# Four convolution taps per channel from TensorE to VectorE, and five weight splits from VectorE to ScalarE and accumulating DMAs

## The chip, the core and the metric

The kernel runs on one core of a Trainium2 chip. The core has a matrix engine (TensorE, "PE" in the profile, with its weight loads as "PEld"), a vector engine (VectorE, "DVE"), an engine for activation functions (ScalarE, "ACT"), a general engine (GpSimd, "POOL") and a synchronisation engine (SyncE, "SP"). SP, ACT and POOL issue DMA transfers, which 16 DMA engines carry out between the chip's main memory (DRAM) and the on-chip memory (SBUF). TensorE's results go into accumulator memory (PSUM), which the kernel uses as eight banks of 128 partitions by 512 numbers of f32. Each engine runs its own list of instructions in order and waits on semaphores for the others.

The metric is the device time of one execution in microseconds, as a median over runs.

## The reference

One transformer block over 256 tokens with 1024 features, all in f32. Attention and a depthwise convolution run side by side on the normalised input, their outputs are joined and projected, and a gated feed-forward layer follows.

```
u = rms_norm(x, mix_norm_g)
q, k, v, glu_a, glu_g = split(u @ w_in)                # 5 x 512 columns
attn_out = causal attention, 8 heads of 64, relative position bias
y = glu_a * sigmoid(glu_g)
y = depthwise causal convolution(y, 31 taps per channel) + b_dw    # 512 channels
conv_out = silu(layer_norm(y))
h = x + concat(attn_out, conv_out) @ w_out
u = rms_norm(h, ffn_norm_g)
h = h + (silu(u @ w_gate) * (u @ w_up)) @ w_down       # 1024 -> 2816 -> 1024
out = rms_norm(h, final_norm_g)
```

With 256 tokens and blocks of 256, each query only sees its own block, so the selection of blocks in the reference has no effect.

## The kernel before

**Split products.** Every large product is made of three TensorE passes in the type f32r. An f32 operand is split into an upper part, which is the operand rounded to f32r, and a lower part, which is what the rounding left. For weights the upper part is `wh`, made from the loaded tile `raw` on ScalarE (the step `h`, function `high`), and the lower part is `wl = raw - wh`, made by a subtraction on VectorE (the step `w`, function `split`, which makes the upper part too where no `h` came before). The input has the parts `uh` and `ul`. The passes are `wh*uh`, `wh*ul` and `wl*uh`. A weight load is a pair of tiles of 128 partitions by 1024 columns, numbered 0 and 1, so that the step `w.v1.0` splits the first tile of the second load of value weights. The names of loads are `a0`, `a1` (the convolution's inputs), `qk0` to `qk3`, `v0`, `v1`, `o0` to `o3` (the output projection), and then `g`, `u`, `d` for the feed-forward layer.

**Memory for weights.** There are six `raw` tiles, so that a load waits until the tiles of three loads earlier are read for the last time. `wl` is one region with nine slots that are used in turn, and there are nine `wh` tiles.

**The convolution.** It has two halves of 256 channels, and each half has two chunks of 128 channels, called j = 0 and 1. The first 20 taps (4*Q with Q = 5) run on TensorE. For that the gated input is stored to DRAM and read back four times with shifts of one token, so that 32 channels times four taps fill the 128 partitions (`ustk`). A stationary operand `wstk` of 128 rows by 32 columns holds the four taps of 32 channels, and one matmul with 256 moving columns adds four taps for 32 channels. `wstk` is built by VectorE in the step `cw`. One chunk takes Q passes times four groups of 32 channels, which is 20 matmuls, into the bank `pc` (the steps `c.half.j`). The other 11 taps (`ONV`) run as single instructions of 128 by 256: tap 0 on ScalarE (step `ca`), taps 1 to 10 as a fused multiply-add on VectorE into `cacc` (steps `ct.half.from.to`). The step `co` adds `pc` to `cacc` and sums the two chunks into `s4` ("s" in the profile) for the layer norm. `l.1` and `l.2` finish the sum, take the mean over channels with a matmul (`pm`) and subtract it from `cacc`.

**Attention.** `qk.hp.j` multiplies for a pair of heads, `qo` scales the result out of PSUM on VectorE, `sc` makes the scores (`ps`), `t` adds the bias and takes the row minimum on VectorE (`lg`, `mn`) and the exponential on ScalarE (`p`), `n` normalises, `fl` transposes on TensorE (`pt`), `fo` copies the transposes (`pts`). The value product is `v.0` to `v.3` (`pv`): `v.2` reads the tile `v1.0`, and `v.3` the tile `v1.1`. `pv.hp` multiplies with the values (`po`), and `mo.hp` splits the result into `mh` on ScalarE and `ml` on VectorE. The output projection `o.k` (`py`) takes 24 matmuls for each k. `o.0` and `o.1` read `o0.0` and `o0.1`, and `o.2` reads `o1.0`.

**What sets the order.** The string `PROGRAM` lists the steps of this part by hand, and each step appends its instructions to the lists of the engines that it uses. All engines keep this order. After it comes the feed-forward loop (`pf`, `pd`), which makes up the rest of the time. There the transfers of POOL move the activations through DRAM (`fd`, `fb`, `hd`, `ht`). In the stage that the change touches, POOL issues no transfer after the two stores of the gated input (`ud`) until the feed-forward layer, and SP issues all weight loads.

## Time and profile before

| | |
|---|---|
| time, median of 3 runs | 283.68 us (283.18 to 284.09) |
| the profiled execution: its time | 283.44 us |
| the profiled execution: its span from first to last instruction | 281.7 us |
| busy: TensorE, VectorE, ScalarE, GpSimd | 273.3, 203.0, 156.4, 43.6 us |
| granted TensorE clock, mean | 0.996 |
| DMA | 63.73 MB, mean 226 GB/s |

All places in time are microseconds from the start of the span of the profiled execution. In a row of the timeline the columns are start, duration, engine, line, operation, output and inputs, shapes, and the number of instructions merged into the row. In square brackets stands the idle time of the engine ahead of the row and what ended it. The start of a row reaches a little into the row before, since instructions overlap, so the pace of an engine is read from the starts. A matmul with f32 operands that aren't f32r, as in the convolution, shows as two records. The windows view gives the busy time of each engine in a stretch of time with the number of instructions, the granted clock, the mean busy share of the DMA engines and their rate.

The steps that the change touches lie between 44 and 86 us.

### The profile page before, as it was taken

The page shows a single profiled execution, that of the slowest core. Times are in us where ns is not written, and L with a number is a line of the kernel's source. Part 1 is how long each engine was busy: PE and PEld are TensorE (multiplying, and loading weights), DVE is VectorE, ACT ScalarE, POOL GpSimd, SP SyncE. Part 2 cuts the span into 40 slices and gives each one's busy share as a digit, 9 for nine tenths or more (in the row PEclk, how much of TensorE's full clock was granted, in tenths as well). Part 3 has the DMA queues.
Part 4 walks back from the last instruction along what each step waited for, and adds up shares of the span by engine and source line. Part 5 has one row for each costly group of instructions (what it writes and reads, how often), then busy time and mean ns, then how long its engine had stood idle before and what let it go on. Part 6 is the DMA issues. An engine that isn't in the chain of part 4 may idle for free.

```text
span 281.7 us, 4726 instructions
## 1 busy us (share of the span) xinstructions
PE 273.3 (97%) x1717; PEld 243.1 (86%) x1717; DVE 203.0 (72%) x375; ACT 156.4 (56%) x272; POOL 43.6 (15%) x80
## 2 busy tenths in 40 slices
...
GB/s 204 364 406 321 278 252 244 357 264 78 0 152 284 110 202 155 303 354 245 340 314 205 323 153 323 285 255 399 245 226 245 308 143 329 158 77 0 0 67 82
DMA packets 22089, 63.73 MB, mean 226 GB/s; under 512 B 3178, under 2 KB 5938, under 8 KB 22066
## 3 DMA queue, kind: packets, MB, share of 16 engines
q1 hardware_dynamic: 18754, 54.94, 59.2%
...
q8 instruction: 13, 0.21, 0.3%
...
## 4 chain that ended last, share of the span: by engine, by line
PE 82%; DVE 9%; issue 3%; DMA 1%; ACT 1%; SPq 1%; POOLq 0%; POOL 0%; DVEq 0%; ACTq 0%
PE pf L74 38%; PE pd L74 18%; PE pqk L74 8%; PE py L74 8%; PE pa L74 3%; PE pg L74 3%; DVE cacc L85 3%; DVE wl L85 2%; PE pc L74 2%; DMA raw_a<-in_w_in 1%; DVE acch L85 1%; PE pv L74 1%; DVE ht L85 1%; PE pt L77 1%; DVE lg L85 1%
## 5 line engine op out<-in xcount | busy, mean ns | idle before, releaser
L74 PE MATMUL pf<-wl,us 128*128 128x512 f32 x176 | 66.7, 379 | 0.0
L74 PE MATMUL pf<-wh_u,us 128*128 128x512 f32 x176 | 54.4, 379 | 0.0
L74 PE MATMUL pf<-wh_g,us 128*128 128x512 f32 x176 | 54.2, 379 | 0.0
L85 DVE TENSOR_TENSOR ff<-fs,pf 128x256 f32<-128x256 f32 x22 | 9.1, 420 | 49.4 <-ACT fs L85 49.4
L85 ACT ACTIVATE fs<-pf,rc_h 128x256 f32<-128x256 f32 x22 | 10.3, 473 | 60.8 <-PE pf L74 59.4
L74 PEld LDWEIGHTS pf<-wl,us 128*128 128x128 f32 x176 | 33.3, 189 | 4.7
L74 PEld LDWEIGHTS pf<-wh_g,us 128*128 128x128 f32 x176 | 33.3, 189 | 4.7
L74 PEld LDWEIGHTS pf<-wh_u,us 128*128 128x128 f32 x176 | 33.3, 189 | 4.7
L74 PE MATMUL pd<-wh_d,fh 128*128 128x512 f32 x84 | 32.0, 381 | 0.0
L74 PE MATMUL pd<-wh_d,fl 128*128 128x512 f32 x84 | 31.9, 380 | 0.0
L74 PE MATMUL pd<-wl,fh 128*128 128x512 f32 x84 | 31.8, 379 | 0.0
...
L85 DVE TENSOR_TENSOR wl<-raw_u,wh_u 128x1024 fp32r<-128x1024 f32 x22 | 26.3, 1219 | 4.9 <-ACT wh_u L85 4.9
L85 ACT CAST wh_u<-raw_u 128x1024 fp32r<-128x1024 f32 x22 | 22.6, 1045 | 11.1 <-PE pf L74 9.0
L85 DVE TENSOR_TENSOR wl<-raw_g,wh_g 128x1024 fp32r<-128x1024 f32 x22 | 25.9, 1217 | 1.1 <-ACT wh_g L85 1.0
L85 DVE TENSOR_TENSOR wl<-raw_d,wh_d 128x1024 fp32r<-128x1024 f32 x22 | 25.6, 1203 | 0.5 <-ACT wh_d L85 0.5
L85 ACT CAST wh_g<-raw_g 128x1024 fp32r<-128x1024 f32 x22 | 21.9, 1044 | 0.0
L85 ACT CAST wh_d<-raw_d 128x1024 fp32r<-128x1024 f32 x22 | 21.8, 1041 | 0.0
L74 PE MATMUL pqk<-us,wh_qk 128*128 128x256 f32 x128 | 21.7, 276 | 0.0
L74 PEld LDWEIGHTS pqk<-us,wh_qk 128*128 128x128 f32 x128 | 19.5, 192 | 0.5 <-issue 0.4
L74 PEld LDWEIGHTS pd<-wh_d,fl 128*128 128x128 f32 x84 | 15.9, 189 | 2.4 <-DVE fl L85 0.2
L74 PE MATMUL py<-mh,wh_o 128*128 128x256 f32 x64 | 18.0, 281 | 0.0
...
## 6 DMA issues: line engine op xcount, KB each, us to landing
...
```

Of the source, the lines that this page charges most:

```text
L74: return tc.keep_in_program_order(nc.tensor.matmul(*args, **kw))
L77: return tc.keep_in_program_order(nc.tensor.transpose(o, i, ident))
L85: return lambda *a, **k: tc.keep_in_program_order(f(*a, **k))
```

## The change

The first half of the convolution runs four passes of four taps on TensorE (16 taps) in place of five (20 taps). The four taps per channel that are left over run on VectorE, as eight more multiply-adds of 128 by 256 (four taps for two chunks). The second half stays as it was. The table of tap columns grows by four taps, so that its load has 172 columns in place of 156, and `wstk` of the first half is built with 512 columns per chunk in place of 640.

Five weight tiles (`v1.0`, `v1.1`, `o0.0`, `o0.1`, `o1.0`) get their lower parts by a new step `x` (`split_by_dma`). ScalarE makes the upper part as before. Then it writes the negated raw tile into the tile's slot of `wl`. The slot has the type f32r, so that what stands there is the negated upper part. Then a DMA that POOL issues adds the raw tile to it, which gives `raw - wh`. The five subtractions on VectorE are gone. The steps stand in the program one after the other behind `w.qk3.1`, where before only `h.v1.0` stood; the others were spread up to `w.o1.0`.

The place in the program where VectorE finishes the first half of the convolution, begins the second, and goes on to the logits of the third pair of heads (`lg`). `upad_81` and `upad_82` are the gated inputs of the two halves. Before:

```order
L85 SCALAR_TENSOR_TENSOR cacc<-upad_81,pv,cacc 128x256 x2
L85 TENSOR_TENSOR cacc<-pc_712,cacc 128x256 x2
L85 TENSOR_TENSOR s_149<-cacc 128x256
L85 TENSOR_TENSOR wl<-raw_v_0_609,wh_v_0_833 128x1024
L85 TENSOR_TENSOR wl<-raw_v_1_610,wh_v_1_834 128x1024
L85 SCALAR_TENSOR_TENSOR cacc<-upad_82,pv,cacc 128x256 x4
L85 TENSOR_TENSOR qk_918<-pqk_860,rb 128x512
L85 TENSOR_TENSOR wl<-raw_o_0_806,wh_o_0_887 128x1024
L85 TENSOR_TENSOR wstk_84<-pv 128x640 x2
L85 SCALAR_TENSOR_TENSOR cacc<-upad_82,pv,cacc 128x256 x4
L85 ISA lg_952,mn_953<-ps_940,bias 128x128
```

And in the changed kernel:

```order
L86 SCALAR_TENSOR_TENSOR cacc<-upad_81,pv,cacc 128x256 x10
L86 TENSOR_TENSOR cacc<-pc_712,cacc 128x256 x2
L86 TENSOR_TENSOR s_149<-cacc 128x256
L86 SCALAR_TENSOR_TENSOR cacc<-upad_82,pv,cacc 128x256 x4
L86 TENSOR_TENSOR qk_925<-pqk_864,rb 128x512
L86 TENSOR_TENSOR wstk_84<-pv 128x640 x2
L86 SCALAR_TENSOR_TENSOR cacc<-upad_82,pv,cacc 128x256 x4
L86 ISA lg_962,mn_963<-ps_950,bias 128x128
```

Eight more taps stand ahead of the sum with `pc`, and three subtractions are gone, two of them ahead of the scaling of `qk` and one behind it.

The place where VectorE goes from the layer norm's sum to the lower parts of the attention output (`ml`), which the output projection waits for. Before:

```order
L85 TENSOR_TENSOR s_149<-cacc 128x256
L85 TENSOR_TENSOR s_149<-s_149 128x256
L85 TENSOR_SCALAR vt<-pv_843,rc_x 128x512
L85 TENSOR_TENSOR wl<-raw_o_1_807,wh_o_1_888 128x1024
L85 TENSOR_TENSOR cacc<-cacc,pm 128x256 x4
L85 TENSOR_TENSOR wl<-raw_o_0_856,wh_o_0_1049 128x1024
L85 TENSOR_TENSOR ml<-po_1116,mh 128x256
```

And in the changed kernel:

```order
L86 TENSOR_TENSOR s_149<-cacc 128x256
L86 TENSOR_TENSOR s_149<-s_149 128x256
L86 TENSOR_SCALAR vt<-pv_847,rc_x 128x512
L86 TENSOR_TENSOR cacc<-cacc,pm 128x256 x4
L86 TENSOR_TENSOR ml<-po_1121,mh 128x256
```

The other two subtractions stood between the sum and `ml`, and are gone.

The place on ScalarE between the transposes of the first two pairs of heads and the exponentials of the third (`p`). Before:

```order
L85 CAST wh_v_0_833<-raw_v_0_609 128x1024
L85 CAST wh_v_1_834<-raw_v_1_610 128x1024
L85 CAST wh_o_0_887<-raw_o_0_806 128x1024
L85 CAST wh_o_1_888<-raw_o_1_807 128x1024
L85 ACTIVATE p_956,sm<-lg_952,mn_953 128x128
```

And in the changed kernel:

```order
L86 CAST wh_v_0_825<-raw_v_0_609 128x1024
L86 ACTIVATE wl<-raw_v_0_609 128x1024
L86 CAST wh_v_1_826<-raw_v_1_610 128x1024
L86 ACTIVATE wl<-raw_v_1_610 128x1024
L86 CAST wh_o_0_889<-raw_o_0_798 128x1024
L86 ACTIVATE wl<-raw_o_0_798 128x1024
L86 CAST wh_o_1_890<-raw_o_1_799 128x1024
L86 ACTIVATE wl<-raw_o_1_799 128x1024
L86 CAST wh_o_0_927<-raw_o_0_860 128x1024
L86 ACTIVATE wl<-raw_o_0_860 128x1024
L86 ACTIVATE p_966,sm<-lg_962,mn_963 128x128
```

Five negations are new, one behind each cast, and the cast of `o1.0` has moved up here from behind the third pair's normalisation. On POOL the five accumulating DMAs stand behind the two stores of the gated input, and ahead of the power function of the convolution's layer norm (`rc_ln`).

The diff; the host code changes only in the number of tap columns that it lays out:

```diff
-ONV = TAPS - 4 * Q
+QH = (4, 5)
+ONV = TAPS - 4 * min(QH)
...
-c.0.0 ct.0.6.7 h.qk3.0 w.v0.0 n.0 n.1 c.0.1 w.v0.1 h.qk3.1 w.qk3.0 ct.0.7.8 ct.0.8.10 qk.2.1 qo.2 ld.o0 fl.0 fo.0 fl.1 fo.1 w.qk3.1 h.v1.0 ct.0.10.11 co.0 w.v1.0
-v.0 ld.o1 qk.3.0 h.v1.1 w.v1.1 h.o0.0 ct.1.1.3 qk.3.1 qo.3 h.o0.1 w.o0.0 cw.1.0 cw.1.1 ct.1.3.5 v.1 sc.2 sc.3 t.2 t.3 ld.o2
-c.1.0 ct.1.5.7 n.2 n.3 c.1.1 ct.1.7.9 ct.1.9.11 h.o1.0 co.1 l.1 v.2 v.3 fl.2 fl.3 vt w.o0.1 fo.2 fo.3 l.2 ld.o3 w.o1.0
+c.0.0 ct.0.6.7 h.qk3.0 w.v0.0 n.0 n.1 c.0.1 w.v0.1 h.qk3.1 w.qk3.0 ct.0.7.8 ct.0.8.10 qk.2.1 qo.2 ld.o0 fl.0 fo.0 fl.1 fo.1 w.qk3.1 x.v1.0 x.v1.1 ct.0.10.15 co.0
+v.0 ld.o1 qk.3.0 x.o0.0 x.o0.1 ct.1.1.3 qk.3.1 qo.3 x.o1.0 cw.1.0 cw.1.1 ct.1.3.5 v.1 sc.2 sc.3 t.2 t.3 ld.o2
+c.1.0 ct.1.5.7 n.2 n.3 c.1.1 ct.1.7.9 ct.1.9.11 co.1 l.1 v.2 v.3 fl.2 fl.3 vt fo.2 fo.3 l.2 ld.o3
...
+    def split_by_dma(name, n):
+        if (name, n) not in made:
+            high(name, n)
+        raw, wh, wl, c = upper[name][n]
+        act.activation(wl[:, c], raw[:, c], AF.Copy, scale=-1.0)
+        pool.dma_start(wl[:, c], raw[:, c], accum_op=ALU.add)
...
     def conv_weights(half, j):
-        n = 4 * Q
-        fold, cw = pv[:, PV_FOLD:PV_N], pv[:, PV_CW + (2 * half + j) * n :]
+        qs = QH[half]
+        fold, cw = pv[:, PV_FOLD:PV_N], pv[:, PV_CW + (2 * half + j) * 4 * Q :]
...
     def conv_tap(c, n):
-        u = upad[c // 2][:, c % 2 * UW + 4 * Q + n : c % 2 * UW + 4 * Q + n + S]
-        w = col(PV_T, n * CC + c)
+        t = 4 * QH[c // 2] + n
+        u = upad[c // 2][:, c % 2 * UW + t : c % 2 * UW + t + S]
+        w = col(PV_T, (t - TAPS + ONV) * CC + c)
...
     def conv(half, j):
...
-        for q in range(Q):
+        qs = QH[half]
+        for q in range(qs):
             for g in range(4):
-                mm(pc[half][32 * g : 32 * g + 32, j * S : (j + 1) * S], wstk[half][:, (4 * j + g) * Q + q],
+                mm(pc[half][32 * g : 32 * g + 32, j * S : (j + 1) * S], wstk[half][:, (4 * j + g) * qs + q],
                    ustk[half][:, g, j * UW + 4 * q : j * UW + 4 * q + S],
-                   start=j == 0 and q == 0, stop=q == Q - 1, skip_group_check=True)
+                   start=j == 0 and q == 0, stop=q == qs - 1, skip_group_check=True)
```

More of the change, by code (lines that the diff above doesn't have):

```diff
@@ L235, in conv_weights @@
     def conv_weights(half, j):
-        n = 4 * Q
-        fold, cw = pv[:, PV_FOLD:PV_N], pv[:, PV_CW + (2 * half + j) * n :]
+        qs = QH[half]
+        fold, cw = pv[:, PV_FOLD:PV_N], pv[:, PV_CW + (2 * half + j) * 4 * Q :]
         vec.tensor_tensor(
-            wstk[half][:, j * n : j * n + n],
-            bass.AP(tensor=fold.tensor, offset=fold.offset, ap=[fold.ap[0], [0, n], [1, 32]]),
-            bass.AP(tensor=cw.tensor, offset=cw.offset, ap=[cw.ap[0], [1, n], [0, 32]]), op=ALU.mult)
+            wstk[half][:, j * 4 * qs : (j + 1) * 4 * qs].rearrange("p (g q) m -> p g q m", g=4),
+            bass.AP(tensor=fold.tensor, offset=fold.offset, ap=[fold.ap[0], [0, 4], [0, qs], [1, 32]]),
+            bass.AP(tensor=cw.tensor, offset=cw.offset, ap=[cw.ap[0], [Q, 4], [1, qs], [0, 32]]), op=ALU.mult)
     def rstd(acc, n, eps, name, b):
@@ L569, in a0 @@
         a_mm(0, k, f"a0_{k // 4 * 4}", k % 4 * 512)
-    ops = {"ld": fetch, "zd": bias_out, "bd": bias_in, "ud": stack_out, "us": stack_in, "h": high, "w": split, "rb": row_scale, "hb": bias_parts, "pl": late_columns, "pz": bias_mm, "zs": bias_copy, "vt": v_out, "rs": scale_x, "rd": scale_diagonal, "ca": lambda half: conv_taps(half, 0, 1),
+    ops = {"ld": fetch, "zd": bias_out, "bd": bias_in, "ud": stack_out, "us": stack_in, "h": high, "w": split, "x": split_by_dma, "rb": row_scale, "hb": bias_parts, "pl": late_columns, "pz": bias_mm, "zs": bias_copy, "vt": v_out, "rs": scale_x, "rd": scale_diagonal, "ca": lambda half: conv_taps(half, 0, 1),
            "a0": a0, "a1": a1, "glu": glu, "qk": qk_mm, "qo": qk_out, "sc": score, "t": logits, "n": normed, "fl": flip,
```

2 lines of the change are left out of this document (1 added, 1 removed).

## The prediction

> **What bounds the kernel now.** I read the page first, then the waits of TensorE, then the timelines of TensorE, VectorE and ScalarE around the change.
>
> ```profile
> PE 273.3 (97%) x1717; PEld 243.1 (86%) x1717; DVE 203.0 (72%) x375; ACT 156.4 (56%) x272; POOL 43.6 (15%) x80
> PE 82%; DVE 9%; issue 3%; DMA 1%; ACT 1%; SPq 1%; POOLq 0%; POOL 0%; DVEq 0%; ACTq 0%
> ```
>
> TensorE is busy for 97% of the span. The chain that ended last gives 9% to VectorE, so it could be that VectorE sets the pace somewhere. The waits of TensorE from 40 to 116 us answer that: there is a single one.
>
> ```profile
> PE py L74 <- DVE ml L85: 0.2, 1, 0.2
> ```
>
> TensorE's timeline in this stage (`pc` is the convolution, the first half at 44.34 and the second at 65.03):
>
> ```profile
> 44.34 4.52 PE L74 MATMUL pc<-ustk,wstk 128*32 128x256 f32 x80
> 48.79 0.49 PE L74 MATMUL pqk<-us,wh_qk 128*128 128x256 f32 x2
> ...
> 63.52 1.58 PE L74 MATMUL ps<-qk 64*128 64x128 f32 x16
> 65.03 4.52 PE L74 MATMUL pc<-ustk,wstk 128*32 128x256 f32 x80
> ...
> 69.81 0.38 PE L74 MATMUL pv<-wl,us 128*128 128x512 f32 x1
> ...
> 72.39 0.38 PE L74 MATMUL pv<-wl,us 128*128 128x512 f32 x1
> ...
> 76.08 0.60 PE L74 MATMUL pm<-s,invc 128*128 128x256 f32 x2
> ...
> 79.36 0.38 PE L74 MATMUL py<-mh,wh_o 128*128 128x256 f32 x1
> 79.98 0.38 PE L74 MATMUL py<-ml,wh_o 128*128 128x256 f32 x1 [0.24 <-DVE ml L85]
> 80.19 0.28 PE L74 MATMUL py<-mh,wl 128*128 128x256 f32 x1
> ```
>
> Every row of that timeline, those left out here too, follows the one before without a gap up to 79.98. So TensorE bounds this stage, and VectorE, which is nearly as full, costs 0.24 us once. Work taken off TensorE shortens the program if nothing that TensorE waits for comes later than its new, earlier time. Work taken off VectorE is worth 0.24 us by itself.
>
> **TensorE's part of the change.** The first half's matmuls go from 40 to 32. From 44.34 to the next row's start at 48.79 are 4.45 us, which is 0.111 us for a matmul (two records). Eight fewer are 0.89 us. From here to the wait at 79.98 every TensorE time below is the one before less 0.89, behind it less 1.13.
>
> **VectorE's part.**
>
> ```profile
> 57.05 2.35 DVE L85 TENSOR_TENSOR wl<-raw_v,wh_v 128x1024 fp32r<-128x1024 f32 x2
> 59.32 1.66 DVE L85 SCALAR_TENSOR_TENSOR cacc<-upad,pv,cacc 128x256 f32<-128x256 f32 x4
> 61.03 0.69 DVE L85 TENSOR_TENSOR qk<-pqk,rb 128x512 f32<-128x512 f32 x1
> 61.64 1.22 DVE L85 TENSOR_TENSOR wl<-raw_o,wh_o 128x1024 fp32r<-128x1024 f32 x1
> 62.77 1.55 DVE L85 TENSOR_TENSOR wstk<-pv 128x640 f32<-128x640 f32 x2
> 64.25 1.67 DVE L85 SCALAR_TENSOR_TENSOR cacc<-upad,pv,cacc 128x256 f32<-128x256 f32 x4
> 65.83 0.28 DVE L85 CUSTOM_DVE_ANT_0 lg<-ps,bias 128x128 f32<-128x128 f32 x1
> ...
> 74.91 0.42 DVE L85 TENSOR_TENSOR s<-s 128x256 f32<-128x256 f32 x1
> ...
> 75.91 1.22 DVE L85 TENSOR_TENSOR wl<-raw_o,wh_o 128x1024 fp32r<-128x1024 f32 x1
> 77.04 1.41 DVE L85 TENSOR_TENSOR cacc<-cacc,pm 128x256 f32<-128x256 f32 x4
> 78.37 1.22 DVE L85 TENSOR_TENSOR wl<-raw_o,wh_o 128x1024 fp32r<-128x1024 f32 x1
> 79.50 1.41 DVE L85 TENSOR_TENSOR ml<-po,mh 128x256 fp32r<-128x256 f32 x4
> ```
>
> By the distance of starts a subtraction is 1.13 us (61.64 to 62.77) and a tap 0.395 (64.25 to 65.83, four of them). The change adds 8 x 0.395 = 3.16 and takes 5 x 1.13 = 5.65. The new taps come first, and only two subtractions fall away beside them. So the scaling of `qk` would come 3.16 - 2.27 = 0.89 later; the 0.13 for which VectorE waited ahead of it (59.32 + 1.58 = 60.90 against 61.03) absorbs part, and it starts at 61.8 and is done by 62.4. TensorE needs it for the second pair's scores, in the middle of the row at 63.52, which is now 63.4. That holds by a microsecond. `wstk` for the second half follows at once and its first chunk is done by 63.2, while TensorE wants it at 65.08 - 0.89 = 64.2. With the third subtraction gone the logits (`lg`) start at 65.83 + 0.76 - 1.13 = 65.46, which is 0.37 earlier. The sum for the layer norm (`s` at 74.91, done 75.33) is ready at 74.96, and TensorE wants it for `pm` at 76.08 - 0.89 = 75.19. This is the closest place: 0.23 us.
>
> The last two subtractions stood ahead of `ml`. Now `ml` comes behind the four subtractions of `pm`: `pm` ends at about 75.8, they take 1.33, and VectorE is free at 77.1. ScalarE delivers `mh` by 77.53 + 0.37 - 0.89 = 77.0 (row below). TensorE wants `ml` at 78.5. So the wait of 0.24 us goes, and nothing takes its place on VectorE.
>
> **ScalarE's part.**
>
> ```profile
> 53.96 2.00 ACT L85 CAST wh_v<-raw_v 128x1024 fp32r<-128x1024 f32 x2
> 55.86 1.05 ACT L85 CAST wh_o<-raw_o 128x1024 fp32r<-128x1024 f32 x1
> 57.88 1.07 ACT L85 CAST wh_o<-raw_o 128x1024 fp32r<-128x1024 f32 x1 [0.97 <-DMA raw_o<-in_w_out]
> 66.22 0.40 ACT L85 ACTIVATE p<-lg,mn 128x128 f32<-128x128 f32 x1 [7.27 <-DVE mn L85]
> ...
> 74.38 0.69 ACT L85 ACTIVATE vt<-pv,rc_x 128x512 f32<-128x512 f32 x1
> ...
> 77.53 0.37 ACT L85 CAST mh<-po 128x256 fp32r<-128x256 f32 x1 [0.60 <-PE po L74]
> ```
>
> A cast takes 0.95 us from start to start (53.96 to 55.86 for two). No row shows a negation of 1024 columns. Below it is bounded by the cast, 0.95, and above by twice the activation of 512 columns at 74.38, 1.38. I take 1.0, since both read and write like the cast. Ten operations from 53.96 on end at 63.7 (65.7 at the upper bound), and the exponentials start at 66.22 - 0.37 = 65.85. So five negations and the cast of `o1.0` fit into the 7.27 us in which ScalarE waited. The tile `o1.0` has to be there at 61.8; its load follows that of `o0.1`, for which ScalarE waited until 57.88, and 0.52 MB more at the rate of 396 GB/s below are 1.3 us, so at 59.2.
>
> **The accumulating DMAs.** POOL issues one when each negation ends: about 55.9, 57.9, 59.8, 61.8 and 63.7. POOL has nothing else there:
>
> ```profile
> 86.46 0.73 POOL L85 TENSOR_TENSOR rc_ln<-ms_ln,mhalf 128x2 f32<-128x2 f32 x1 [50.21 <-DVE ms_ln L85]
> ```
>
> TensorE needs the results at 69.81 - 0.89 = 68.9 (`v1.0`), 72.39 - 0.89 = 71.5 (`v1.1`), 80.19 - 1.13 = 79.1 (`o0.0`), about 81.8 (`o0.1`) and 84.9 (`o1.0`), by this row of the chain of waits, in which `o.2` begins at 85.83 and a block of 24 matmuls takes 2.79:
>
> ```profile
> 85.83 2.79 PE py L74 x24
> ```
>
> No row shows an accumulating transfer. The nearest are these: POOL's four stores of 256 KB (`hd`) in the feed-forward layer, with the instruction that waited for the last, and the landing of the eight `raw_o` loads of 512 KB; and how busy the DMA engines are in two stretches of this stage.
>
> ```profile
> 176.66 0.58 POOL L85 DMA_DIRECT2D hd<-hb  x1 [0.76 <-DVE hb L85]
> ...
> 186.10 1.13 POOL L85 DMA_DIRECT2D ht<-hd  x2 [6.90 <-DMA hd<-hb]
> ```
>
> ```profile
> DMA to landing us min/median/max: 3.3/4.3/8.0
> ```
>
> ```profile
> 55.00:58.00 3.00, 3.00 (x26) 2.92 (x26) 2.97 (x7) 2.03 (x4) 0.00 (x0) 1.00 1.03 396
> ...
> 70.00:76.00 6.00, 6.00 (x35) 5.34 (x34) 5.93 (x19) 5.20 (x12) 0.00 (x0) 1.00 0.00 0
> ```
>
> Let a tile take t, one behind the other from 55.9. The lower bound is the full rate of 396 GB/s at 55 to 58, which gives 0.52 MB in 1.3 us. The stores took 9.44 us for four of 256 KB beside weight loads, which is 4.7 for 512 KB. An accumulation also reads its destination; if that doubles the slow row, t is 9.4, the upper bound. The five deadlines ask t below 13.0, 7.8, 7.7, 6.5 and 5.8. I take 3.0, between the full rate and the stores, nearer to the stores than to their double, since the DMA engines stand still from 70 to 76 and the loads of the stage end soon after 60. Then the last tile lands at 71, 14 us before its use. The loads of `o2` and `o3` now wait for the accumulations, which have to read `raw`, and not for subtractions at 57.05 and later; with t at 3.0 the first is free at 59, as before, and the last by 71, where its subtraction ended at 79.50.
>
> The Trainium skill bears on this in "Collectives: The Full Stack", section "The bandwidth ceiling: the fold count and why AG ≠ RS ≠ AR". It states that an add inside a DMA engine costs two source reads, about 31 GB/s per engine for a copy and half of it for the reduction. As an estimate from that page, 16 engines at half of 31 give 250 GB/s and t = 2.1. The sum would be the same as with 3.0, and no run so far shows the accumulation.
>
> **The sum.** 0.89 from the convolution and 0.24 from the wait are 1.13 us. Behind 80 us TensorE runs on to the feed-forward layer with no wait, so the rest moves as a whole. The profiled execution took 283.44 (its span 281.7), and would take 282.3; against the median of 283.68, 0.24 more, I forecast **282.6**, with 0.05 for the tight place at `pm`.
>
> **The rivals.** A measurement of this kernel tells a change from none at about 0.3%, 0.85 us, and the forecast of 1.1 is only just beyond.
>
> 1. *Part of the gain leaks.* The taps make VectorE late where its slack is 0.23 us. If `s` comes 0.65 later than worked out, which is 0.28 later than before, `pm` waits 0.42 of it, and 0.7 us are left: 283.0. Eight taps and the logits at a pace a few per cent worse, or exponentials that start late because of the negations, would do that. For it speaks that VectorE has no idle time ahead of `s` to catch up in; against it, that all its rows here repeat within a few hundredths.
>
> 2. *The accumulations are slow,* and TensorE waits for `wl` of `o1.0`. This decides from t = 5.8 on, and with t = 6.2 the kernel is slower than before by more than the measurement tells (55.9 + 31.0 = 86.9, 2.0 behind 84.9). Midway between the stores and their double, t = 7.1, the last lands at 91.4, 6.5 behind: 282.6 + 6.5 = 289.1. For it speaks that the operation has no row at all and that the stores were far below the full rate; against it, that the stores ran beside full weight traffic and the accumulations mostly don't.
>
> 3. *POOL cannot write its descriptors while VectorE is busy.* Then the first accumulation starts in VectorE's first gap, and lands as the `raw_o` loads did, after 3.3 to 8.0 us.
>
> ```profile
> 67.23 0.29 DVE L85 CUSTOM_DVE_ANT_0 lg<-ps,bias 128x128 f32<-128x128 f32 x1 [0.21 <-ACT p L85]
> ```
>
> The gap ahead of 67.23 comes at 66.7 now, so `v1.0` lands at 70.0 to 74.7 and TensorE loses 1.1 to 5.8: 286.1 in the middle. Against it speaks that POOL's 40 issues of `fb`, beside a VectorE that is busy for 72% of the span, took from 582 to 604 ns each.
>
> ```profile
> L85 POOL DMA_DIRECT2D fb<-fd x40: 582/582/604, 123.5 to 250.7; - x40
> ```
>
> The Trainium skill states in "SBUF — State Buffer", section "Who interferes with whom", that GpSimd is locked out of a port shared with VectorE during some VectorE operations and cannot write descriptors then; by that rule this rival would hold, and the row of `fb` does not agree.
>
> **How the numbers follow.** The forecast has 0.53, with its own range of 282.0 to 282.8; rival 1 has 0.27, rival 2 0.15, rival 3 0.05. Faster by over 0.3%: the forecast, less a little for those runs that fall short, 0.52. Within 0.3%: 0.28. Slower: 0.20. The range begins at 281.9, the full 1.13 with half the spread of the runs shown beside it, and ends at 285.5, which takes in rival 1 and the mild cases of 2 and 3 and leaves out most of their rest.
>
> **What would show it.** Right: `pc` of the first half with 64 records in 3.6 us, no wait of TensorE at `py`, `pm` unmoved against its neighbours, and accumulations that land before 68.9 and 71.5. Wrong: a wait of TensorE for a DMA ahead of `pv` or `py` (rival 2 or, with late issues on POOL, rival 3), a wait at `pm` or `pt` (rival 1), or `lg` waiting for ScalarE, which would mean negations above 1.4 us.

## The result and the profile after

The changed kernel took 282.28 us (median; 281.92 to 282.46) against 283.69 for the kernel before in the same comparison: the ratio is 0.9944, with a 95% interval of 0.9931 to 0.9957. So it is faster by 1.41 us, and the whole interval lies beyond the 0.3% that can be told from no change. The forecast was 282.6. In this comparison the profiled execution of the changed kernel took 1629.55 us, with TensorE busy for 1620.7 us in place of 272.1, so the profile after is that of the repeat, `e1_changed`, whose profiled execution took 282.35 us.

The page of the changed kernel (busy time by engine, and the shares of the chain that ended last) and the waits of TensorE:

```profile
PE 272.1 (97%) x1701; PEld 241.9 (86%) x1701; DVE 200.5 (71%) x378; ACT 160.7 (57%) x277; POOL 48.2 (17%) x85
PE 89%; DVE 3%; issue 3%; DMA 2%; ACT 1%; SPq 1%; POOLq 0%; POOL 0%; DVEq 0%; ACTq 0%
```

```profile
PE wm L75 <- POOL ones L86: 1.0, 1, 1.0
PE pa L75 <- ACT us L86: 0.3, 1, 0.3
PE pa L75 <- DVE wl L86: 0.2, 1, 0.2
```

TensorE has 16 records less (1701 for 1717). VectorE's share of the chain fell from 9% to 3% and TensorE's rose from 82% to 89%. The waits that are left lie in the start-up, ahead of the first row below; the one at `py` is gone, and none for an accumulation has come.

Starts in the chain that ended last give the size of the gain, free of what the start-up does from run to run (the first `pc` starts anywhere from 44.1 to 45.4 us in the kernel before and the experiments): from the first `pc` to `ps_ln`, the first thing behind the block of `py` that had the wait. First before, then changed (start, length, what):

```profile
44.41 4.45 PE pc L74 x80
...
85.49 0.34 PE ps_ln L74 x4
```

```profile
44.53 3.59 PE pc L75 x64
...
64.36 4.45 PE pc L75 x80
...
84.24 0.34 PE ps_ln L75 x4
```

The distance was 41.08 us and is 39.71: 1.37 less. The convolution gives 0.86 of it (4.45 to 3.59), so 0.51 is left for the wait, where the prediction had 0.24. The starts around the wait say the same. TensorE's timeline of the changed kernel:

```profile
75.34 0.60 PE L75 MATMUL pm<-s,invc 128*128 128x256 f32 x2
...
78.61 0.38 PE L75 MATMUL py<-mh,wh_o 128*128 128x256 f32 x1
78.83 0.28 PE L75 MATMUL py<-ml,wh_o 128*128 128x256 f32 x1
78.94 0.28 PE L75 MATMUL py<-mh,wl 128*128 128x256 f32 x1
```

From the first `py` to the third are 0.33 us here. Before, it was 80.19 - 79.36 = 0.83. The difference is 0.50. The bracket [0.24 <-DVE ml L85] in the row of before counts idle time only from the modelled end of the matmul ahead, and consecutive matmuls start well ahead of that end: here the second starts 0.22 after the first, which is shown as 0.38 long.

VectorE in the changed kernel, from the new taps to `ml`:

```profile
55.26 4.04 DVE L86 SCALAR_TENSOR_TENSOR cacc<-upad,pv,cacc 128x256 f32<-128x256 f32 x10
...
61.92 0.69 DVE L86 TENSOR_TENSOR qk<-pqk,rb 128x512 f32<-128x512 f32 x1
...
65.58 0.29 DVE L86 CUSTOM_DVE_ANT_0 lg<-ps,bias 128x128 f32<-128x128 f32 x1
...
74.67 0.43 DVE L86 TENSOR_TENSOR s<-s 128x256 f32<-128x256 f32 x1
...
77.30 0.96 DVE L86 TENSOR_TENSOR ml<-po,mh 128x256 fp32r<-128x256 f32 x2
```

`s` is done at 75.10 and TensorE begins `pm` at 75.34, so 0.24 us are left at the place that the prediction called the closest. `ml` begins at 77.30, where it began at 79.50.

ScalarE, a cast, the next cast with one negation between them, and the first exponential:

```profile
54.08 1.05 ACT L86 CAST wh_v<-raw_v 128x1024 fp32r<-128x1024 f32 x1
...
55.99 1.05 ACT L86 CAST wh_v<-raw_v 128x1024 fp32r<-128x1024 f32 x1
...
65.97 0.40 ACT L86 ACTIVATE p<-lg,mn 128x128 f32<-128x128 f32 x1 [2.27 <-DVE mn L86]
```

Cast and negation together take 1.91, so a negation is 0.96. ScalarE still waits 2.27 us for VectorE ahead of the exponentials, so the negations delay nothing. GpSimd's first and last accumulating DMA, and the first and last landing (KB each, then us from issue to landing):

```profile
56.40 0.92 POOL L86 DMA_DIRECT2D wl<-raw_v  x1 [20.03 <-ACT wl L86]
...
63.99 0.86 POOL L86 DMA_DIRECT2D wl<-raw_o  x1 [1.03 <-ACT wl L86]
```

```profile
wl<-raw_v POOLq DMA_DIRECT2D x1, 512.0 KB, 5.6
```

```profile
wl<-raw_o POOLq DMA_DIRECT2D x1, 512.0 KB, 12.8
```

They land from 62.0 to 76.8, so one tile takes (76.8 - 62.0) / 4 = 3.7 us on average. The first is wanted behind the second half's `pc`, at 64.36 + 4.45 = 68.8, and is some 7 us early; the last is wanted by the block behind `ps_ln`, at 84.6, and is 7.8 us early.

### The profile page after: what moved, and what is told of

It reads as the page before. It is cut to its first block, busy times and chain, and to the rows that moved or that the text cites. A ratio compares the mean times of both kernels' runs of the same rounds, so it can differ in the third digit from the quotient of the medians.

```text
span 1627.8 us, 4712 instructions
## 1 busy us (share of the span) xinstructions
PE 1620.7 (100%) x1701; PEld 1233.4 (76%) x1701; DVE 203.7 (13%) x378; ACT 163.2 (10%) x277; POOL 48.2 (3%) x85
## 4 chain that ended last, share of the span: by engine, by line
PE 98%; issue 2%; DVE 0%; POOL 0%; POOLq 0%; DVEq 0%
PE pf L75 43%; PE pd L75 19%; PE py L75 8%; PE pqk L75 8%; PE pa L75 4%; PE pv L75 4%; PE pg L75 4%; PE pc L75 3%; PE pt L78 1%; PE ps L75 1%; PE po L75 1%; PE wm L75 1%; PE pe L75 0%; PE pb_x L75 0%; PE pb_ln L75 0%
## 5 line engine op out<-in xcount | busy, mean ns | idle before, releaser
L75 PE MATMUL pf<-wl,us 128*128 128x512 f32 x176 | 300.3, 1706 | 0.0
L75 PE MATMUL pf<-wh_u,us 128*128 128x512 f32 x176 | 271.3, 1709 | 0.0
L75 PE MATMUL pf<-wh_g,us 128*128 128x512 f32 x176 | 270.7, 1707 | 0.0
L75 PEld LDWEIGHTS pf<-wh_u,us 128*128 128x128 f32 x176 | 162.9, 926 | 69.3 <-issue 69.3
L75 PEld LDWEIGHTS pf<-wh_g,us 128*128 128x128 f32 x176 | 162.7, 925 | 69.3 <-issue 68.9
L75 PEld LDWEIGHTS pf<-wl,us 128*128 128x128 f32 x176 | 162.9, 926 | 68.8 <-issue 68.8
L75 PE MATMUL pd<-wh_d,fh 128*128 128x512 f32 x84 | 144.0, 1715 | 0.0
L75 PE MATMUL pd<-wl,fh 128*128 128x512 f32 x84 | 143.3, 1706 | 0.0
L75 PE MATMUL pd<-wh_d,fl 128*128 128x512 f32 x84 | 143.2, 1704 | 0.0
L75 PE MATMUL pqk<-us,wh_qk 128*128 128x256 f32 x128 | 109.2, 1046 | 0.0
```

The costliest lines, as they stand in the source:

```text
L75: return tc.keep_in_program_order(nc.tensor.matmul(*args, **kw))
```

## The experiments

The theory is the prediction's: 0.89 us from eight matmuls, and the end of the one wait at `py`, because TensorE bounds the stage and the other engines stay in time. What was open is the size of the second term, whether each half of the change does its part alone, and how far the accumulations are from hurting.

**e1_changed: the changed kernel again.** No edit.

> The changed kernel again, for a profile whose TensorE runs at its usual pace. My theory, TensorE alone sets the gain: 8 matmuls of the convolution (0.89 us) and the wait at the output projection (0.24 us), so 282.4 to 282.6, TensorE's start of the feed-forward layer (first pf, 102.39 before) at 101.3, and the last row of the feed-forward layer earlier by the same amount. The rival, the gain is larger than 1.1 us because a second place moves too (the first runs gave 1.4 us): then 282.0 to 282.3, and the distance to the kernel before grows from 1.1 us ahead of 100 us to 1.4 or more behind it. The five accumulations land before TensorE needs them by either.

Measured: 282.36 against 283.79, ratio 0.9953 (0.9936 to 0.9971), a gain of 1.43. A third comparison, `e10_changed`, which stood beside the kernel `e9_gated`, gave 282.47 against 283.64, 0.995 (0.9932 to 0.9969), 1.17; its distance from the first `pc` to `ps_ln` is again 39.71.

> The changed kernel once more, beside the run above on the same chip. My theory, by the starts on TensorE: 0.89 us from the convolution and 0.51 from the wait, 1.4 us below the kernel before. The rival, the 1.13 of the forecast.

What follows: 1.2 to 1.4 us by the medians, 1.37 in both traces. From `ps_ln` to the end of the span all the experiments take the same 196.1 to 196.4 us (the kernel before 196.2), so the gain arises in the stage, and the rival's second place behind 100 us was not found.

**e2_conv_only: the taps without the relief.** The convolution of the changed kernel, with the five subtractions back on VectorE:

```diff
-c.0.0 ct.0.6.7 h.qk3.0 w.v0.0 n.0 n.1 c.0.1 w.v0.1 h.qk3.1 w.qk3.0 ct.0.7.8 ct.0.8.10 qk.2.1 qo.2 ld.o0 fl.0 fo.0 fl.1 fo.1 w.qk3.1 x.v1.0 x.v1.1 ct.0.10.15 co.0
-v.0 ld.o1 qk.3.0 x.o0.0 x.o0.1 ct.1.1.3 qk.3.1 qo.3 x.o1.0 cw.1.0 cw.1.1 ct.1.3.5 v.1 sc.2 sc.3 t.2 t.3 ld.o2
-c.1.0 ct.1.5.7 n.2 n.3 c.1.1 ct.1.7.9 ct.1.9.11 co.1 l.1 v.2 v.3 fl.2 fl.3 vt fo.2 fo.3 l.2 ld.o3
+c.0.0 ct.0.6.7 h.qk3.0 w.v0.0 n.0 n.1 c.0.1 w.v0.1 h.qk3.1 w.qk3.0 ct.0.7.8 ct.0.8.10 qk.2.1 qo.2 ld.o0 fl.0 fo.0 fl.1 fo.1 w.qk3.1 h.v1.0 ct.0.10.15 co.0 w.v1.0
+v.0 ld.o1 qk.3.0 h.v1.1 w.v1.1 h.o0.0 ct.1.1.3 qk.3.1 qo.3 h.o0.1 w.o0.0 cw.1.0 cw.1.1 ct.1.3.5 v.1 sc.2 sc.3 t.2 t.3 ld.o2
+c.1.0 ct.1.5.7 n.2 n.3 c.1.1 ct.1.7.9 ct.1.9.11 h.o1.0 co.1 l.1 v.2 v.3 fl.2 fl.3 vt w.o0.1 fo.2 fo.3 l.2 ld.o3 w.o1.0
```

> The convolution's part alone: 16 taps of the first half on TensorE, eight more taps on VectorE, and all weight splits on VectorE in their old places. My theory, VectorE has no room in this stage: 3.16 us more ahead of the scaling of the last qk, of which 0.13 is absorbed, so scores, wstk, the sum for pm and ml come about 3.0 us later and TensorE waits for them: 286.4 to 286.8, slower. The rival, VectorE's load was not near the limit: TensorE's 0.89 us are kept, 282.8.

Measured: 286.99 against 283.79, ratio 1.0101 (1.0082 to 1.0119): slower by 3.2 us. TensorE's waits, and VectorE's scaling and first logits of the third pair:

```profile
PE ps L75 <- DVE qk L86: 1.2, 1, 1.2
...
PE pc L75 <- DVE wstk L86: 0.9, 1, 0.9
```

```profile
65.10 0.68 DVE L86 TENSOR_TENSOR qk<-pqk,rb 128x512 f32<-128x512 f32 x1
...
69.89 0.28 DVE L86 CUSTOM_DVE_ANT_0 lg<-ps,bias 128x128 f32<-128x128 f32 x1
```

`qk` begins 4.07 later than before (61.03) and the logits 4.06 later (65.83). But 1.03 of this is the start-up of this execution, whose first `pc` starts at 45.37 in the timeline where it started at 44.34. So the taps make VectorE 3.04 later, close to the 3.16 less 0.13 that were expected, and TensorE's distance from the first `pc` to `ps_ln` grows by 3.06, to 44.14 (in the chain, where `ps_ln` begins at 89.58 and starts of `pc` lie 0.07 behind the timeline's). VectorE has no room for eight taps with the five subtractions in these places, and TensorE's shorter convolution is lost in the waits for it.

**e3_splits_only: the relief without the taps.** The five tiles by ScalarE and DMA, the convolution as before:

```diff
-QH = (4, 5)
+QH = (5, 5)
...
-c.0.0 ct.0.6.7 h.qk3.0 w.v0.0 n.0 n.1 c.0.1 w.v0.1 h.qk3.1 w.qk3.0 ct.0.7.8 ct.0.8.10 qk.2.1 qo.2 ld.o0 fl.0 fo.0 fl.1 fo.1 w.qk3.1 x.v1.0 x.v1.1 ct.0.10.15 co.0
+c.0.0 ct.0.6.7 h.qk3.0 w.v0.0 n.0 n.1 c.0.1 w.v0.1 h.qk3.1 w.qk3.0 ct.0.7.8 ct.0.8.10 qk.2.1 qo.2 ld.o0 fl.0 fo.0 fl.1 fo.1 w.qk3.1 x.v1.0 x.v1.1 ct.0.10.11 co.0
```

> The splits' part alone: 20 taps of the first half on TensorE as before, the five tiles split by ScalarE and accumulating DMAs. My theory: only the wait of 0.24 us at the output projection goes, 283.4, not to be told from before. The rival, the part of the gain that the sum lacked comes from VectorE's relief: 283.0 or less.

Measured: 283.17 against 283.79, ratio 0.9979 (0.9969 to 0.9989): 0.62 us. By the bracket's 0.24 it would have been 283.55, so the larger price is the right one. The chain of waits:

```profile
44.60 4.45 PE pc L75 x80
...
85.17 0.34 PE ps_ln L75 x4
```

The distance is 40.57, 0.51 less than before. With the 0.86 of the convolution that is exactly the 1.37 of the whole change. On TensorE the two terms add up; as changes of the kernel they don't, since the taps alone lose 3.06.

**e5_one_move: the wait alone.** The kernel before, with the one subtraction that stood directly ahead of `ml` moved; nothing goes to ScalarE or DMA:

```diff
-c.1.0 ct.1.5.7 n.2 n.3 c.1.1 ct.1.7.9 ct.1.9.11 h.o1.0 co.1 l.1 v.2 v.3 fl.2 fl.3 vt w.o0.1 fo.2 fo.3 l.2 ld.o3 w.o1.0
-pv.0 mo.0 pv.1 mo.1 l.6 pv.2 mo.2 pv.3 mo.3 l.3 w.o1.1 ld.g0 w.o2.0 w.o2.1 ld.u0 o.0 o.1 l.7 w.o3.0 o.2 h.o3.1 ld.g1 l.4 l.5 w.o3.1 w.g0.0 o.3 w.g0.1 o.4
+c.1.0 ct.1.5.7 n.2 n.3 c.1.1 ct.1.7.9 ct.1.9.11 h.o1.0 co.1 l.1 v.2 v.3 fl.2 fl.3 vt w.o0.1 fo.2 fo.3 l.2 ld.o3
+pv.0 mo.0 pv.1 mo.1 w.o1.0 l.6 pv.2 mo.2 pv.3 mo.3 l.3 w.o1.1 ld.g0 w.o2.0 w.o2.1 ld.u0 o.0 o.1 l.7 w.o3.0 o.2 h.o3.1 ld.g1 l.4 l.5 w.o3.1 w.g0.0 o.3 w.g0.1 o.4
```

> The kernel before, with one subtraction moved: the one of o1.0 goes from ahead of ml to behind the first two ml, where nothing waits for it soon. Nothing else changes, so this is the wait at the output projection by itself. My theory after the first runs: the wait costs what the starts of the two matmuls show, 79.36 to 79.98, less the usual 0.11 between two starts: 0.51 us, so 283.3, and the second py follows the first in about 0.2 us. The rival, the number in the square brackets is the cost: 0.24 us, 283.55.

Measured: 283.31 against 283.85, ratio 0.9978 (0.9963 to 0.9994), 0.54 us. TensorE's timeline:

```profile
79.32 0.38 PE L74 MATMUL py<-mh,wh_o 128*128 128x256 f32 x1
79.53 0.28 PE L74 MATMUL py<-ml,wh_o 128*128 128x256 f32 x1
79.64 0.28 PE L74 MATMUL py<-mh,wl 128*128 128x256 f32 x1
```

First to third in 0.32 us instead of 0.83, and the distance from the first `pc` to `ps_ln` is 40.57 as in `e3_splits_only`. This is the cleanest measurement of the disputed term: one step of the order moved, everything else as before, and the wait is worth 0.51. It also shows that this part of the gain needs no DMA at all. The expectation came to 0.51 by taking 0.11 as the usual distance of the first two `py`; it is 0.21 here, and the 0.10 that this leaves out is the third one's, which came 0.21 behind the second before and comes 0.11 behind it here.

**e6_two_back: three tiles instead of five.** The changed kernel with `o0.1` and `o1.0` back on VectorE at their old places, ahead of `ml`:

```diff
-v.0 ld.o1 qk.3.0 x.o0.0 x.o0.1 ct.1.1.3 qk.3.1 qo.3 x.o1.0 cw.1.0 cw.1.1 ct.1.3.5 v.1 sc.2 sc.3 t.2 t.3 ld.o2
-c.1.0 ct.1.5.7 n.2 n.3 c.1.1 ct.1.7.9 ct.1.9.11 co.1 l.1 v.2 v.3 fl.2 fl.3 vt fo.2 fo.3 l.2 ld.o3
+v.0 ld.o1 qk.3.0 x.o0.0 ct.1.1.3 qk.3.1 qo.3 h.o0.1 cw.1.0 cw.1.1 ct.1.3.5 v.1 sc.2 sc.3 t.2 t.3 ld.o2
+c.1.0 ct.1.5.7 n.2 n.3 c.1.1 ct.1.7.9 ct.1.9.11 h.o1.0 co.1 l.1 v.2 v.3 fl.2 fl.3 vt w.o0.1 fo.2 fo.3 l.2 ld.o3 w.o1.0
```

> The changed kernel with the last two of the five tiles (o0.1 and o1.0) split on VectorE again, in their old places; three tiles stay with ScalarE and the accumulating DMAs. My theory: the three relieve VectorE ahead of the logits by just what the taps add, so all of TensorE's 0.89 us arrive at pm, but ml comes at about 79.1 and the second py at 79.6, where the changed kernel had it at 78.8: 0.8 us of the gain are lost, 283.1. The rival, the two tiles' relief is only worth the 0.24 us of the brackets: 282.6.

Measured: 283.53 against 283.85, ratio 0.9981 (0.9965 to 0.9998), 0.32 us. TensorE:

```profile
78.20 0.38 PE L75 MATMUL py<-mh,wh_o 128*128 128x256 f32 x1
79.32 0.38 PE L75 MATMUL py<-ml,wh_o 128*128 128x256 f32 x1 [0.74 <-DVE ml L86]
79.53 0.28 PE L75 MATMUL py<-mh,wl 128*128 128x256 f32 x1
```

First to third `py` are 1.33 us, 1.00 more than without a wait; the bracket says 0.74. The convolution's gain runs into VectorE: the distance from the first `pc` to `ps_ln` is 84.83 - 44.12 = 40.71, only 0.37 less than before. So the two last tiles are not a bonus beside the convolution. They are what lets its 0.86 us through, and without them the loss at the wait grew from 0.51 to 1.00. The expectation had the mechanism and put the loss at 0.8; the time lies 0.4 above the 283.1 that it gave.

**e4_plain_copy: what the accumulation costs as a transfer.** The DMA overwrites its destination instead of adding to it:

```diff
-        pool.dma_start(wl[:, c], raw[:, c], accum_op=ALU.add)
+        pool.dma_start(wl[:, c], raw[:, c])
```

> The changed kernel with plain copies of raw into wl in place of the accumulations: the lower parts are left out (wl holds the raw tile), so only the times of the transfers count. My theory of an accumulation as two reads for one write: the copies land one behind the other at half the distance or less of the accumulations (about 1.3 to 2 us a tile against 3 to 4), and the kernel's time is that of the changed kernel, since neither is waited for. The rival, the transfer is bound by its issue or its fixed latency: both land after the same time.

Measured (one execution): 282.37, the same as with the accumulation, so its price is fully hidden. The first three copies land at 61.7, 63.0 and 64.2, 1.2 to 1.3 us apart as the theory asked, and the last two at 69.7 and 73.0, with weight loads between them; the accumulations landed at 62.0, 64.4, 68.3, 73.0 and 76.8. In the stretch from 59 to 62 us hardly any load runs in either kernel. Its rows (busy time of the engines, then the clock, the DMA share and GB/s), first with the plain copies, then in the changed kernel with the stretch behind it:

```profile
59.00:62.00 3.00, 3.00 (x21) 2.79 (x20) 2.96 (x9) 3.00 (x4) 0.54 (x1) 1.00 1.07 400
```

```profile
59.00:62.00 3.00, 3.00 (x21) 2.79 (x20) 2.96 (x9) 3.00 (x4) 1.05 (x2) 1.00 1.03 199
62.00:65.00 3.00, 3.00 (x36) 1.98 (x39) 3.00 (x7) 1.69 (x2) 1.72 (x2) 1.00 1.05 184
```

The DMA engines are full in all three rows, and move half as much while they accumulate. GpSimd takes 0.86 to 0.92 us to issue an accumulation and 0.54 to 0.55 for a copy. The Trainium skill states in "Collectives: The Full Stack", section "The bandwidth ceiling: the fold count and why AG ≠ RS ≠ AR", that the add of a reduction between cores needs two source reads, so that it runs at half the rate of a copy; the ratio agrees here (199 or 184 against 400). The estimate of 250 GB/s that the prediction worked out from that page is above what was measured.

**e8_twice: twice the accumulations.** The negation with a factor of -2, and a second accumulation for each tile:

```diff
-v.0 ld.o1 qk.3.0 x.o0.0 x.o0.1 ct.1.1.3 qk.3.1 qo.3 x.o1.0 cw.1.0 cw.1.1 ct.1.3.5 v.1 sc.2 sc.3 t.2 t.3 ld.o2
+v.0 ld.o1 qk.3.0 x.o0.0 x.o0.1 ct.1.1.3 qk.3.1 qo.3 x.o1.0 y.v1.0 y.v1.1 y.o0.0 y.o0.1 y.o1.0 cw.1.0 cw.1.1 ct.1.3.5 v.1 sc.2 sc.3 t.2 t.3 ld.o2
...
-        act.activation(wl[:, c], raw[:, c], AF.Copy, scale=-1.0)
+        act.activation(wl[:, c], raw[:, c], AF.Copy, scale=-2.0)
         pool.dma_start(wl[:, c], raw[:, c], accum_op=ALU.add)
+    def add_again(name, n):
+        raw, wh, wl, c = upper[name][n]
+        pool.dma_start(wl[:, c], raw[:, c], accum_op=ALU.add)
```

> The changed kernel with each of the five accumulations done twice: ScalarE writes minus two times raw, and POOL adds raw a second time to each tile behind the five first additions (so the lower parts come out doubled). This doubles the suspected cost and puts the first tile's second addition behind all the others. My theory, the accumulations are hidden only by their slack of 7 us: at 3.7 us a tile, the first tile lands at about 80.5 where TensorE needs it at 69.1, and the fifth at 95; TensorE loses 11 to 13 us ahead of v.2, and the time is 293 to 296. The rival, the additions are bound by something that overlaps (latency, not the engines' rate), so that ten take little longer than five: under 288.

Measured (one execution): 290.42, 6.6 above the kernel before (283.85) and so 8.0 above the changed one. This lies between the two expectations. TensorE stalls once:

```profile
68.60 0.48 PE L75 MATMUL pv<-wh_v,us 128*128 128x512 f32 x1
75.11 0.80 PE L75 MATMUL pv<-wl,us 128*128 128x512 f32 x1 [6.03 <-DMA wl<-raw_v]
```

So rival 2 exists as a mechanism, and doubling the traffic brings it on. The stall was shorter than expected, because the first seven landings, from 62.5 to 77.5, are 2.5 us apart on average while hardly any load runs beside them, against 3.8 to 4.7 for those of the changed kernel that shared the DMA engines with loads. But it explains only 6 of the 8 us: from the `pv` at 75.11 to the next `pt` are 7.01 us, where the changed kernel takes 4.97. These 2 us are in the granted clock, the last number but two of each row:

```profile
72.00:75.00 3.00, 0.00 (x0) 0.00 (x0) 2.87 (x8) 0.99 (x3) 0.87 (x1) 0.54 1.06 205
75.00:78.00 3.00, 2.89 (x7) 2.35 (x8) 0.00 (x0) 0.00 (x0) 0.00 (x0) 0.50 1.06 205
78.00:81.00 3.00, 3.00 (x13) 2.53 (x12) 0.00 (x0) 0.00 (x0) 0.00 (x0) 0.82 1.04 209
```

The idle time began at 69.1. From about 72 on the clock was at half, and it stayed there for some four microseconds after TensorE had work again.

**e7_more_taps: can the next four taps follow?** One more chunk gives four taps to VectorE, GpSimd makes the second half's `wstk` to relieve it, and the logits get a third buffer (its lines are not shown):

```diff
-QH = (4, 5)
+QC = (4, 4, 4, 5)
...
-w.a1_1.1 w.qk0.0 bd ld.qk2 a1.2 rb glu.0 ud.0 w.qk0.1 ld.v0 us.0 a1.3 w.qk1.0 w.qk1.1 ca.0 glu.1 ud.1 ld.qk3 us.1
+w.a1_1.1 w.qk0.0 bd ld.qk2 a1.2 rb glu.0 ud.0 w.qk0.1 ld.v0 us.0 a1.3 w.qk1.0 w.qk1.1 ca.0 glu.1 ud.1 ld.qk3 us.1 cw.1.0 cw.1.1
-v.0 ld.o1 qk.3.0 x.o0.0 x.o0.1 ct.1.1.3 qk.3.1 qo.3 x.o1.0 cw.1.0 cw.1.1 ct.1.3.5 v.1 sc.2 sc.3 t.2 t.3 ld.o2
-c.1.0 ct.1.5.7 n.2 n.3 c.1.1 ct.1.7.9 ct.1.9.11 co.1 l.1 v.2 v.3 fl.2 fl.3 vt fo.2 fo.3 l.2 ld.o3
+v.0 ld.o1 qk.3.0 x.o0.0 x.o0.1 ct.1.1.3 qk.3.1 qo.3 x.o1.0 ct.1.3.5 v.1 sc.2 sc.3 t.2 t.3 ld.o2
+c.1.0 ct.1.5.7 n.2 n.3 c.1.1 ct.1.7.9 ct.1.9.15 co.1 l.1 v.2 v.3 fl.2 fl.3 vt fo.2 fo.3 l.2 ld.o3
...
-        vec.tensor_tensor(
+        (pool if half else vec).tensor_tensor(
```

> A try for a faster version: in the changed kernel four more taps of the first chunk of the second half go from TensorE to VectorE (four matmuls, 0.44 us), the operand wstk of the second half is built by GpSimd right behind its stores, which takes 1.47 us from VectorE, and the logits get a third buffer, so that VectorE waits less for ScalarE. My theory: VectorE gets 1.58 us of taps and loses 1.8 us, so the sum for pm still comes in time and TensorE's 0.44 us are kept: 281.9. The rival: GpSimd's multiplications hold up VectorE by sharing memory ports, or pm waits since its slack was only 0.24: no gain, 282.3 or more.

Measured: 283.52 against 283.85, ratio 0.9988 (0.9971 to 1.0005). No gain over the kernel before can be told, and it is about 1 us above the changed kernel. GpSimd and VectorE, then VectorE in the changed kernel:

```profile
36.16 2.29 POOL L86 TENSOR_TENSOR wstk<-pv 128x512 f32<-128x512 f32 x2
```

```profile
36.50 4.17 DVE L86 TENSOR_TENSOR wl<-raw_qk,wh_qk 128x1024 fp32r<-128x1024 f32 x2 [0.61 <-ACT wh_qk L86]
...
45.15 0.28 DVE L86 CUSTOM_DVE_ANT_0 lg<-ps,bias 128x128 f32<-128x128 f32 x1
```

```profile
36.73 2.36 DVE L86 TENSOR_TENSOR wl<-raw_qk,wh_qk 128x1024 fp32r<-128x1024 f32 x2 [0.61 <-ACT wh_qk L86]
...
43.91 0.29 DVE L86 CUSTOM_DVE_ANT_0 lg<-ps,bias 128x128 f32<-128x128 f32 x1 [0.26 <-PE ps L75]
```

Two subtractions beside GpSimd's multiplications took 4.17 us instead of 2.36. The first logits came 1.24 later, the exponentials with them, and TensorE's transposes of `p` were drawn out:

```profile
50.93 2.40 PE L78 MATMUL pt<-ident,p 128*128 128x128 f32 x12
```

In the changed kernel, as before, these take 1.47:

```profile
50.83 1.47 PE L78 MATMUL pt<-ident,p 128*128 128x128 f32 x12
```

The waits of TensorE do not list this loss, since it is spread over the twelve. The transposes lose 0.93, the scores ahead of `pc` 0.33 (their row takes 1.91 for 1.58) and `pm` 0.11, and the four matmuls give 0.43 back: 0.94 above the changed kernel by the trace.

**e9_gated: the same multiplications beside another instruction.** A small copy on GpSimd holds them back until VectorE works on the logits, which read one operand from PSUM:

```diff
-w.a1_1.1 w.qk0.0 bd ld.qk2 a1.2 rb glu.0 ud.0 w.qk0.1 ld.v0 us.0 a1.3 w.qk1.0 w.qk1.1 ca.0 glu.1 ud.1 ld.qk3 us.1 cw.1.0 cw.1.1
-qk.0.0 qk.0.1 qo.0 h.qk2.0 h.qk2.1 ca.1 w.qk2.0 w.qk2.1 ct.0.1.3 qk.1.0 ct.0.3.4 ld.v1 qk.1.1 qo.1 h.v0.0 h.v0.1 ct.0.4.6 qk.2.0 sc.0 sc.1 t.0 t.1
+w.a1_1.1 w.qk0.0 bd ld.qk2 a1.2 rb glu.0 ud.0 w.qk0.1 ld.v0 us.0 a1.3 w.qk1.0 w.qk1.1 ca.0 glu.1 ud.1 ld.qk3 us.1
+qk.0.0 qk.0.1 qo.0 h.qk2.0 h.qk2.1 ca.1 w.qk2.0 w.qk2.1 ct.0.1.3 qk.1.0 ct.0.3.4 ld.v1 qk.1.1 qo.1 h.v0.0 h.v0.1 ct.0.4.6 qk.2.0 sc.0 sc.1 t.0 gate cw.1.0 cw.1.1 t.1
...
+    def gate():
+        pool.tensor_copy(gt, mns[0, 0][:, 0:1])
```

> The last kernel of the run before (four more taps to VectorE, wstk of the second half on GpSimd, a third buffer for the logits) with one thing changed: GpSimd waits with its two multiplications until VectorE has made the first row minimum of the logits, at about 44. There VectorE reads PSUM and one operand in SBUF for 2.8 us, where at 36.5 it subtracted two operands in SBUF and took 4.17 us for two in place of 2.36. My theory, the two engines hold each other up only while both read two operands in SBUF: VectorE keeps its pace, the sum for pm is in time, and TensorE gains 0.44 us more than the changed kernel: 0.4 below it. The rival, GpSimd's work holds up VectorE wherever it stands: the logits stretch by 1 us or more, and the time is that of the changed kernel or above it.

Measured: 282.26 against 283.64, ratio 0.9945 (0.9927 to 0.9963). The loss of `e7_more_taps` is gone. GpSimd, and VectorE:

```profile
44.87 2.28 POOL L86 TENSOR_TENSOR wstk<-pv 128x512 f32<-128x512 f32 x2
```

```profile
44.36 0.29 DVE L86 CUSTOM_DVE_ANT_0 lg<-ps,bias 128x128 f32<-128x128 f32 x1 [0.25 <-PE ps L75]
...
46.58 1.24 DVE L86 SCALAR_TENSOR_TENSOR cacc<-upad,pv,cacc 128x256 f32<-128x256 f32 x2
...
68.49 5.19 DVE L86 SCALAR_TENSOR_TENSOR cacc<-upad,pv,cacc 128x256 f32<-128x256 f32 x12
```

All logits keep their pace; only the taps at 46.58, which read two operands from SBUF, are held up (1.24 instead of 0.88 for the two; the second begins at 47.35, GpSimd is done at 47.15). The Trainium skill states in "SBUF — State Buffer", section "Who interferes with whom", that VectorE instructions with two inputs from SBUF contend with GpSimd's reads and those with at most one, outside the two-port modes, don't; these traces agree, in both directions (4.17 for 2.36, and the logits unchanged).

Yet only 0.17 of the 0.43 us that the second half's `pc` is shorter (72 records instead of 80) arrived: the distance to `ps_ln` is 39.54 against 39.71. `pm` takes 0.70 in the chain instead of 0.43, so TensorE waits 0.27 for `s`. The last row holds the reason: four taps of one chunk now stand in a row at its end, and the last three of them each need the one just before. The timeline of single instructions has the starts of the first nine 0.395 apart, those of these three 0.52 behind the one before (72.15, 72.68, 73.20, the one ahead of them at 71.64), and the sum with `pc`, which needs the last, 0.59 behind (73.79). From the first tap to that sum are 5.30 us where twelve at 0.395 are 4.74, so 0.56 are lost.

**e11_interleaved: the four taps spread.** The same work, with the four new taps placed singly between other instructions of VectorE:

```diff
-c.0.0 ct.0.6.7 h.qk3.0 w.v0.0 n.0 n.1 c.0.1 w.v0.1 h.qk3.1 w.qk3.0 ct.0.7.8 ct.0.8.10 qk.2.1 qo.2 ld.o0 fl.0 fo.0 fl.1 fo.1 w.qk3.1 x.v1.0 x.v1.1 ct.0.10.15 co.0
-v.0 ld.o1 qk.3.0 x.o0.0 x.o0.1 ct.1.1.3 qk.3.1 qo.3 x.o1.0 ct.1.3.5 v.1 sc.2 sc.3 t.2 t.3 ld.o2
-c.1.0 ct.1.5.7 n.2 n.3 c.1.1 ct.1.7.9 ct.1.9.15 co.1 l.1 v.2 v.3 fl.2 fl.3 vt fo.2 fo.3 l.2 ld.o3
+c.0.0 ct.0.6.7 h.qk3.0 w.v0.0 n.0 n.1 c.0.1 w.v0.1 h.qk3.1 w.qk3.0 ct.0.7.8 ct.0.8.10 qk.2.1 qo.2 ld.o0 fl.0 fo.0 fl.1 fo.1 w.qk3.1 x.v1.0 x.v1.1 ct.0.10.15 tp.2.11 co.0
+v.0 ld.o1 qk.3.0 x.o0.0 x.o0.1 ct.1.1.3 tp.2.12 qk.3.1 qo.3 x.o1.0 ct.1.3.5 v.1 sc.2 sc.3 t.2 tp.2.13 t.3 ld.o2
+c.1.0 ct.1.5.7 n.2 tp.2.14 n.3 c.1.1 ct.1.7.9 ct.1.9.11 co.1 l.1 v.2 v.3 fl.2 fl.3 vt fo.2 fo.3 l.2 ld.o3
```

> The run before with the four new taps of the second half spread out: there they stood one behind the other on the same chunk and took 5.19 us for twelve, where twelve that alternate between two chunks take 4.74. Now one stands ahead of the first half's sum, one ahead of the scaling of the last qk, one between the two pairs' logits, and one between their reciprocals. Theory: dependent taps of one chunk cost about 0.1 us more each, the sum for pm comes 0.4 us earlier, pm's wait of 0.27 goes, and TensorE keeps the whole 0.44 us: 281.9 to 282.0, 1.8 below the kernel before. The rival, pm waits for something else than VectorE's sum: no change, 282.3.

Measured: 282.18 against 283.81, ratio 0.9947 (0.9934 to 0.996), the lowest median of the study. The chain:

```profile
44.17 3.59 PE pc L75 x64
...
74.71 0.43 PE pm L75 x2
...
83.45 0.34 PE ps_ln L75 x4
```

`pm` is back at 0.43 and the distance is 39.28: the full 0.43 less than in the changed kernel. VectorE does the same work as in `e9_gated`, and its taps beside GpSimd's multiplications still take 1.23, so it is the order of the four taps that made the difference. The third buffer of the logits stands in all three of these kernels and was not tried alone. The medians of the two (282.18; 282.28, 282.36 and 282.47) lie too near for the intervals to separate them, so only the trace shows this last step.

## Why the prediction was right, step by step

- *TensorE bounds the stage, so its eight matmuls count in full.* Right. The 0.89 measured 0.86, and `e2_conv_only` shows that it needs VectorE's relief.
- *The wait of 0.24 us goes, and nothing takes its place.* The mechanism was right and the size wrong: "VectorE, which is nearly as full, costs 0.24 us once". That term measured 0.51, alone in `e5_one_move`, with the whole relief in `e3_splits_only`, and in the changed kernel. The number came from the bracket; the starts in the very rows quoted gave 0.62 between two `py` that otherwise start 0.21 to 0.22 apart, and another 0.10 to the third. The sum with 0.51 is 0.89 + 0.51 = 1.40, and 1.41, 1.43 and 1.17 were measured. This term is why the forecast of 282.6 lay 0.3 above the result.
- *VectorE's times.* `qk` predicted at 61.8 and found at 61.92, the logits at 65.46 and found at 65.58, the slack at `pm` 0.23 and found 0.24. The start-up was 0.12 us later in this execution, which is the difference of the first two. (The 65.08 given for the start of `pc` is 65.03 in the row, which decides nothing.) Rival 1 (the gain leaks at `pm`) did not occur, with 0.24 us to spare. `e9_gated` shows what it looks like: with four dependent taps more, `pm` waits 0.27.
- *ScalarE.* A negation was taken as 1.0 and took 0.96, and ScalarE kept 2.27 us of idle time.
- *The accumulations.* Taken at 3.0 us a tile, with the last landing at 71; it was 2.5 without loads beside them (`e8_twice`), 3.7 on average here, and 76.8. Rival 2 was to decide from 5.8 on, so the choice between the bounds of 1.3 and 9.4 was near enough. That was luck in part, since the reason given for it, that the loads would be over soon after 60, was not borne out: there were hardly any from 59 to 65, and from then on loads that had waited for the first accumulations shared the DMA engines with the last ones. The slack of 7.8 us covered it.
- *Rival 3, GpSimd unable to write descriptors beside a busy VectorE.* It did not occur: the first two issues, at 56.40 and 58.30, took 0.92 and 0.89 us, both inside the ten taps, which kept their 0.4 us each, and the first tile landed at 62.0, while the first gap that VectorE's timeline marks ends at 66.98. The prediction says that by the rule of the Trainium skill this rival would hold. That reads too much into "SBUF — State Buffer", section "Who interferes with whom": it names copies, casts and `tensor_scalar` as the operations that can take the shared port pair whole, and not these taps.
- *Still open.* The third comparison gave 0.2 us less gain than the other two, with the same distance in the trace; no run tells more than that the medians spread so far.
